# Softmax maxima of the selected and sliding branches from one score pass instead of two

## The chip, the cores and the metric

The kernel runs on one core of a Trainium2 chip. A core has five engines with an instruction queue each, worked off in order: PE (TensorE, matrix products into PSUM), DVE (VectorE), ACT (ScalarE), POOL (GpSimd) and SP (which issues the DMAs). PEld is PE's loading of the stationary operand, shown apart. The metric is the device time of one execution in microseconds (us), as a median of runs; lower is better.

## What is computed

A decoder trunk of two residual layers over 1024 positions with 1024 features, each followed by a SwiGLU block. The change concerns the second layer's sparse attention: 8 heads of 64 features in 2 groups, and for each block of 128 queries three branches, of which two matter here:

```python
q0 = qb * Q_BLOCK
s_s = jnp.einsum('bgrqd,bgqkd->bgrqk', qblk, k_sel) * scale      # selected blocks: 8 of 16, chosen per query
p_s = masked_softmax(s_s, sel_mask)
o_slc = jnp.einsum('bgrqk,bgqkd->bgrqd', p_s, v_sel)
s_w = jnp.einsum('bgrqd,bgkd->bgrqk', qblk, k_band) * scale      # sliding window of 512
p_w = masked_softmax(s_w, w_mask)
o_win = jnp.einsum('bgrqk,bgkd->bgrqd', p_w, v_band)
```

`masked_softmax` subtracts the row maximum before the exponential and divides by the sum.

## The kernel before, in words

All work is recorded as operations first. The class `Order` (L112) then puts them into one order for each engine: a list schedule that takes, on the engine that comes free first, the ready operation with the lowest number. That number is the operation's place in the record plus an offset for its phase from the table `SHIFT` (L47). So the order follows from the record, from `Order`'s own costs, and from the offsets. All instructions are issued from one helper line, L379; the profile tells them apart by tile names.

The stage that matters lies between the projection of the queries (PSUM tile `pcq`) and the output projection (PSUM tile `po`). For every query block qb of 0 to 7 it runs:

- `prep(qb)` (L1173): transposes the block's queries (`pqt`), and makes from them the pair `QQ`. Its first half, QH, is the rounded high part of the query, once in partitions 0 to 63 and once in 64 to 127. Its second half, QL, has the low part in partitions 0 to 63; the rows from 64 carry additive terms: the mask of the selection (rows 64 to 79, blocks 4 to 7 only) and the negated maxima (rows 96 to 111). It also does the compressed branch (`sc`, `ecmp`, `ptc`, `pvc`), the selection (`fcmp`, `pbt`) and its mask.
- `smax(qb, g)` (L1264) for both groups g: the scores of each head with the queries as stationary operand go to PSUM tiles `s` (two buffers), by two products for each bank and branch: QH with `K1` (high part of the keys over their low part) and QL with `K2` (high part of the keys, and constant rows for the additive terms). DVE reduces each bank to a maximum (`mx`), POOL writes the maxima to `nmx`, PE transposes that (`pm`), and ACT writes it into rows 96 to 111 of QL.
- `att(qb, g)` (L1329): the scores again, now transposed (`sT`), with both products and so with the maximum already subtracted; ACT takes the exponential (`pT`), PE multiplies by the values (`pv`), DVE scales and adds into `o`.

Into the same stretch falls DVE's share of the convolution branch, taps of 1024 columns on the tiles `y`, of which 54 stand among the attention's instructions. The pool `t4` (L406) has two buffers; in this stage the last user before the attention is `tq` of the query projection.

Of the kernel before, what the change touches and what calls it, by code (L numbers as in the profile page):

```python
# [9 lines left out]
F32 = mybir.dt.float32  # L10
F32R = mybir.dt.float32r
# [7 lines left out]
P = 128  # L19
# [12 lines left out]
H = 8  # L32
G = 2
R = 4
# [358 lines left out]
def trunk(ctx, tc, x, norm_mix, norm_ffn, ffn_gate, ffn_up, ffn_down, w_in_even, conv_a, pool_w,  # L393
          pool_scale, w_out_even, w_in_odd, q_norm, k_norm, cmp_pos, cmp_w1, cmp_w2, conf_dw,
          conf_dw_b, conf_ln_g, conf_ln_b, w_out_odd, cf32, cb16, k2c, out):
    nc = Order(tc)
# [6 lines left out]
    def unit(shape, name, dt=F32):  # L403
        return data.tile(shape, dt, tag="u8", bufs=NU, name=name)

    def t4(shape, name, dt=F32):  # L406
        return data.tile(shape, dt, tag="t4", bufs=NT4, name=name)
# [4 lines left out]
    def t2(shape, name, dt=F32):  # L412
        return data.tile(shape, dt, tag="t2", bufs=NT2, name=name)
# [359 lines left out]
    for i in range(4):  # L773
# [3 lines left out]
        for h in range(2):  # L777
# [19 lines left out]
            pb = ps1([P, 512], "pb")  # L797
# [134 lines left out]
    K1s, K2s = (unit([P, G, T], n, F32R) for n in ("K1s", "K2s"))  # L932
# [130 lines left out]
    K1w, K2w = (unit([P, G, T], n, F32R) for n in ("K1w", "K2w"))  # L1063
# [104 lines left out]
    def bc(a, n):  # L1168
        return a[:, :, None].to_broadcast([P, a.shape[1], n])

    qstate = {}

    def prep(qb):  # L1173

        gts = gates[:, qb].rearrange("p (h t) -> p h t", t=3)
        QQ = unit([P, 2, H, P], "QQ", F32R)
        o = data.tile([P, H, HD], F32, tag="o", bufs=2, name="o")
        qstate[qb] = QQ, o, gts
        QH, QL = QQ[:, 0], QQ[:, 1]
        nc.gpsimd.memset(QL[64:128].bitcast(F32), 0.0)  # L1180
        p = psn([P, 4, P], "pqt")
        for k in range(4):
            nc.tensor.transpose(p[:, k], Q[qb // 4][:, qb % 4, P * k:P * (k + 1)], ident)
        for u in range(2):
            src = p[64 * u:64 * u + 64]
            own = QH[64 * u:64 * u + 64, u::2]
            nc.scalar.copy(own, src)
            nc.scalar.copy(QH[64 - 64 * u:128 - 64 * u, u::2], src)
            nc.vector.tensor_tensor(QL[0:64, u::2], src, own.bitcast(F32), op=ALU.subtract)
            yield  # L1190

        sc = psn([P, R, G, 64], "sc")
# [2 lines left out]
                         start=True, stop=False)  # L1195
        for r in range(R):
            for g in range(G):
                for s in range(2):
                    nc.tensor.matmul(sc[:, r, g], QQ[:, s, g * R + r], (Kc, Kc2)[s][:, g * 64:(g + 1) * 64],
                                     start=False, stop=r == R - 1 and g == G - 1 and s == 1)  # L1200
# [31 lines left out]
        if qb >= 4:  # L1232
            f = t2([P, 512], "fcmp")
            nc.vector.tensor_tensor(f.rearrange("p (h n) -> p h n", h=H), e, bc(st[:, 8:16], 64), op=ALU.mult)
            nc.vector.scalar_tensor_tensor(f, f, FMIN, f, op0=ALU.is_ge, op1=ALU.mult)
            yield
            w = f[:, 0:256]
            acc = f[:, 0:128]
            nc.vector.tensor_tensor(w, f[:, 0:256], f[:, 256:512], op=ALU.add)
            nc.vector.tensor_tensor(acc, f[:, 0:128], f[:, 128:256], op=ALU.add)  # L1240
            imp = f[:, 128:160].rearrange("p (g j) -> p g j", g=G)
            a4 = acc.rearrange("p (g j k) -> p g j k", g=G, k=4)
            nc.vector.tensor_reduce(imp, a4, axis=AX.X, op=ALU.add)
            nc.vector.tensor_tensor(imp[:, :, 1:], imp[:, :, 1:], a4[:, :, 0:15, 3], op=ALU.add)
            yield
            cA = cf[:, None, C_A + 16 * (qb - 4):C_A + 16 * (qb - 3)].to_broadcast([P, G, 16])
            cB = cf[:, None, C_B + 16 * (qb - 4):C_B + 16 * (qb - 3)].to_broadcast([P, G, 16])
            nc.vector.tensor_tensor(imp, imp, cA, op=ALU.mult)
            nc.vector.tensor_tensor(imp, imp, cB, op=ALU.add)
            yield  # L1250
            top = f[:, 160:176].rearrange("p (g j) -> p g j", g=G)
            left = f[:, 192:224].rearrange("p (g j) -> p g j", g=G)
            for g in range(G):
                nc.vector.max(top[:, g], imp[:, g])
                nc.vector.match_replace(left[:, g], top[:, g], imp[:, g], TAKEN)
            nc.vector.tensor_scalar(selx[:, :, 64:80], left, TAKEN, NEG, op0=ALU.not_equal, op1=ALU.mult)
            yield
            pb = psn([96, G, P], "pbt")
            for g in range(G):
                nc.tensor.transpose(pb[:, g], selx[:, g], ident)  # L1260
            for g in range(G):
                nc.scalar.copy(QL[64:80, R * g:R * (g + 1)], pb[64:80, g, None, :].to_broadcast([16, R, P]))

    def smax(qb, g):  # L1264

        QQ = qstate[qb][0]
        mx = sml(24, "mx", "mx").rearrange("p (b c h) -> p b c h", b=2, c=3)
        if qb >= 4:
            banks = [[(0, qb - 1, 1, 2), (1, qb - 4, 4, 2)]]
            m = qb - 1  # L1270
            banks += [[(0, 0, 1, m)]] if m <= 4 else [[(0, 0, 1, m - 3)], [(0, m - 3, 1, 3)]]
            banks.append([(1, qb - 3, 1, 3)])
        elif qb == 2:
            banks = [[(br, 0, 1, 3)] for br in range(2)]
        else:
            w = min(qb + 1, 2)
            banks = [[(br, k0, 1, w) for br in range(2)] for k0 in range(0, qb + 1, w)]
        for r in range(R):
            h = R * g + r
            used = [0, 0]  # L1280
            for bank in banks:
                ps = ps1([P, 512], "s")
                c0 = 0
                masks = []
                for br, k0, step, n in bank:
                    for s in range(2):
                        end = s == 1 and br == bank[-1][0] and not any(
                            k + (m - 1) * d == qb for _, k, d, m in bank)
                        K = ((K1s, K2s), (K1w, K2w))[br][s]
                        k = K[:, g].rearrange("p (b k) -> p b k", k=P)[:, k0:k0 + (n - 1) * step + 1:step]  # L1290
                        nc.tensor.matmul(ps[:, c0:c0 + n * P].rearrange("p (b k) -> p b k", k=P), QQ[:, s, h], k,
                                         start=c0 == 0 and s == 0, stop=end)
                    if step == 4:
                        masks.append((c0, B_EDGE))
                    if k0 + (n - 1) * step == qb:
                        masks.append((c0 + (n - 1) * P, B_DIAG))
                    c0 += n * P
                if masks:
                    lo = masks[0][0]
                    if len(masks) == 3:  # L1300
                        nc.tensor.matmul(ps[:, lo:c0], identb, cb[:, B_DED:B_DED + 3 * P], start=False, stop=True)
                    else:
                        n = len(masks)
                        o_ = ps[:, :c0].rearrange("p (b k) -> p b k", b=n)[:, :, c0 // n - P:]
                        nc.tensor.matmul(o_, identb, cb[:, None, B_DIAG:B_DIAG + P].to_broadcast([P, n, P]),
                                         start=False, stop=True)
                if len(bank) == 2:
                    nc.vector.tensor_reduce(mx[:, :, used[0], r], ps[:, :c0].rearrange("p (b k) -> p b k", b=2),
                                            axis=AX.X, op=ALU.max)
                    used = [used[0] + 1, used[1] + 1]  # L1310
                else:
                    br = bank[0][0]
                    nc.vector.tensor_reduce(mx[:, br, used[br], r:r + 1], ps[:, :c0], axis=AX.X, op=ALU.max)
                    used[br] += 1
                yield
        if used[0] == 3:
            nc.vector.tensor_tensor(mx[:, 0, 1], mx[:, 0, 1], mx[:, 0, 2], op=ALU.max)
        if used[1] == 2:
            nc.vector.tensor_tensor(mx[:, :, 0], mx[:, :, 0], mx[:, :, 1], op=ALU.max)
        nm = nmx[g]  # L1320
        nv = nm[:, 96:112].rearrange("p (b s h) -> p b s h", b=2, s=2)
        nc.gpsimd.tensor_copy(nv[:, :, 0].bitcast(F32R), mx[:, :, 0])
        nc.gpsimd.tensor_tensor(nv[:, :, 1], mx[:, :, 0], nv[:, :, 0], op=ALU.subtract)
        pm = psn([P, P], "pm")
        nc.tensor.transpose(pm, nm, ident)
        for r in range(R):
            nc.scalar.activation(QQ[96:112, 1, R * g + r], pm[96:112], AF.Copy, scale=cf[96:112, C_DEL + r:C_DEL + r + 1])

    def att(qb, g):  # L1329

        QQ, o, gts = qstate[qb]
        w0 = max(0, qb - 4)
        items = [(0, kb, 0) for kb in range(qb + 1)] + [(1, kb, w0) for kb in range(w0, qb + 1)]
        small = qb == NB - 1 and g == 1
# [25 lines left out]
        for j, (br, kb, k0) in enumerate(items):  # L1360
            if kb == k0:
                pv = psb([P, R, HD + 1], "pv")
            for r in range(R):
                nc.tensor.matmul(pv[:, r], pT[j][:, r], V[:, br, kb, 64 * g:64 * g + 65],
                                 start=kb == k0 and r == 0, stop=kb == qb and r == R - 1)
# [110 lines left out]
```

## Time and profile before

| | us |
|---|---|
| median of 3 runs | 2342.45 (2339.01 to 2343.81) |
| profiled execution | 2341.84 |
| its span | 2339.2 |
| PE busy | 2286.6 (98%) |
| DVE busy | 1450.7 (62%) |
| ACT busy | 720.8 (31%) |
| mean granted clock of PE | 0.992 of 2.4 GHz |

2.6 us of the profiled execution lie outside the span. Shares over the whole run hide the stage in question: from 1230 to 1520 us DVE is nearly as busy as PE, while in the SwiGLU blocks on either side PE is full and DVE is not. A matmul's busy time overlaps that of the next one, so its cost in a full queue is the distance between two starts, not its duration.

### The profile page before, as it was taken

How to read it: one execution, taken by the hardware profiler on the slowest of the kernel's cores; microseconds unless marked ns; L12 is line 12 of the kernel's file. 1: busy time of each engine (PE TensorE's matmuls, PEld its weight loads, DVE VectorE, ACT ScalarE, POOL GpSimd, SP SyncE). 2: the span in 40 equal slices, each digit the busy share in tenths (PEclk: the TensorE clock that was granted, in tenths of full speed). 3: DMA queues.
4: the chain of work that ended last, by engine and by line, in shares of the span. 5: the costliest groups of instructions: out<-in, count | busy, mean ns of one | idle time of the engine just before them, and what ended most of it. 6: DMA issues, size and time to landing. Idle time of an engine off the chain costs nothing.

```text
span 2339.2 us, 27505 instructions
## 1 busy us (share of the span) xinstructions
PE 2286.6 (98%) x11047; PEld 1886.9 (81%) x11047; DVE 1450.7 (62%) x2270; ACT 720.8 (31%) x1253; POOL 77.1 (3%) x116
## 2 busy tenths in 40 slices
PE   7999989999999999999999989999899999999999
PEld 6888868888888888877887878988688888888887
DVE  6444386565656543569999988723865656565432
ACT  4221252222223210324334434632522222232100
POOL 0000000000000000001111000000000000000000
PEclk9999999999999999999999999999999999999999
DMA  5113123222326321322200000032231223262312
GB/s 168 54 63 108 72 82 108 63 82 81 99 63 252 108 100 36 104 64 89 71 22 1 1 1 1 15 112 72 81 108 61 84 81 99 63 242 107 102 37 81
DMA packets 160296, 189.53 MB, mean 81 GB/s; under 512 B 6257, under 2 KB 127017, under 8 KB 160169
## 3 DMA queue, kind: packets, MB, share of 16 engines
q1 hardware_dynamic: 160168, 187.78, 24.4%
q8 instruction: 86, 1.41, 0.3%
q14 instruction: 42, 0.34, 0.0%
HBM read 147.91 MB, written 39.85 MB: 80 GB/s over the span
## 4 chain that ended last, share of the span: by engine, by line
PE 90%; DVE 5%; ACT 2%; issue 1%; DMA 1%; POOL 0%; SPq 0%; ACTq 0%; POOLq 0%; DVEq 0%
PE pd L379 21%; PE pu L379 18%; PE pg L379 18%; PE po L379 7%; PE pv L379 4%; PE s L379 3%; PE sT L379 3%; PE pvv L379 2%; PE pp L379 2%; PE pb L379 2%; PE pcc L379 2%; PE pcq L379 2%; PE pca L379 1%; PE pcb L379 1%; PE pbk L379 1%; DVE y L379 1%
## 5 line engine op out<-in xcount | busy, mean ns | idle before, releaser
L379 PE MATMUL pd<-wd,ah 128*128 128x512 f32 x2112 | 491.2, 394 | 0.0
L379 PEld LDWEIGHTS pd<-wd,ah 128*128 128x128 f32 x2112 | 396.6, 188 | 90.7
L379 DVE TENSOR_TENSOR xf<-pd,xf 128x512 f32<-128x512 f32 x192 | 130.1, 689 | 215.5 <-PE pd L379 215.1
L379 DVE SCALAR_TENSOR_TENSOR y<-z,dwv,y 128x1024 f32<-128x1024 f32 x120 | 153.9, 1283 | 0.8
L379 PEld LDWEIGHTS pv<-V,pT 128*128 128x128 f32 x1056 | 142.7, 193 | 5.9 <-ACT pT L379 0.6
L379 PE MATMUL pg<-T,wgc 128*128 128x512 f32 x528 | 133.0, 398 | 11.6 <-ACT T L379 11.6
L379 PE MATMUL pv<-V,pT 128*128 128x65 f32 x1056 | 138.8, 267 | 0.1
L379 PE MATMUL pg<-B,wga 128*128 128x512 f32 x528 | 130.1, 394 | 2.8 <-ACT pgu L379 2.8
L379 ACT CAST wd<-raw 128x1024 fp32r<-128x1024 f32 x44 | 45.1, 1047 | 282.4 <-PE pd L379 179.7
L379 PE MATMUL pu<-B,wua 128*128 128x512 f32 x528 | 129.8, 394 | 0.0
L379 PE MATMUL pu<-T,wuc 128*128 128x512 f32 x528 | 129.6, 393 | 0.0
L379 PEld LDWEIGHTS pg<-T,wgc 128*128 128x128 f32 x528 | 99.9, 190 | 36.2 <-ACT T L379 12.5
L379 PEld LDWEIGHTS pg<-B,wga 128*128 128x128 f32 x528 | 98.9, 188 | 26.2 <-ACT pgu L379 3.6
L379 PEld LDWEIGHTS pu<-T,wuc 128*128 128x128 f32 x528 | 99.2, 188 | 23.0
L379 PEld LDWEIGHTS pu<-B,wua 128*128 128x128 f32 x528 | 99.0, 188 | 23.2 <-DVE wua L379 0.3
L379 ACT ACTIVATE pT<-sT 128x512 f32<-128x512 f32 x132 | 77.3, 596 | 103.0 <-PE sT L379 102.1
L379 DVE TENSOR_TENSOR act<-pg,pgu 128x512 f32<-128x512 f32 x66 | 45.6, 691 | 91.2 <-PE pg L379 91.0
L379 DVE TENSOR_TENSOR puu<-pu,puu 128x512 f32<-128x512 f32 x88 | 60.9, 692 | 62.9 <-PE pu L379 62.9
L379 DVE TENSOR_REDUCE mx<-s 128x2 f32<-128x512 f32 (+3 forms) x160 | 92.8, 592 | 11.1 <-PE s L379 8.8
L379 PE MATMUL po<-woo,mB 128*128 128x512 f32 x384 | 91.6, 396 | 0.0
L379 PE MATMUL po<-woe,mA 128*128 128x512 f32 x384 | 90.9, 395 | 0.0
L379 PEld LDWEIGHTS po<-woe,mA 128*128 128x128 f32 x384 | 71.6, 188 | 15.9
(331 smaller groups left out, 3957.9 us busy)
## 6 DMA issues: line engine op xcount, KB each, us to landing
raw<-in_ffn_gate_dram SPq DMA_DIRECT2D x44, 512.0 KB, 4.0
rawp<-in_ffn_up_dram SPq DMA_DIRECT2D x44, 512.0 KB, 5.1
actd<-act SPq DMA_DIRECT2D x44, 512.0 KB, 3.0
raw<-in_ffn_down_dram SPq DMA_DIRECT2D x44, 512.0 KB, 4.4
ad<-actd SPq DMA_DIRECT2D x44, 512.0 KB, 6.9
raw<-in_w_in_even_dram SPq DMA_DIRECT2D x16, 512.0 KB, 4.4
xf<-xm SPq DMA_DIRECT2D x8, 1024.0 KB, 10.7
raw<-in_w_in_odd_dram SPq DMA_DIRECT2D x16, 512.0 KB, 3.6
```

The lines of the kernel that those rows point to most:

```text
L379: getattr(getattr(nc, op.eng), op.name)(*op.args, **op.kw)
```

## The change

In `smax`, the maxima are taken from one product for each bank and branch: QH with `K1` for the sliding branch, and for the selected branch of blocks 0 to 3. For the selected branch of blocks 4 to 7 the mask has to be in the scores, so a third form of the queries is made, `QM`: the high part in rows 0 to 63, the selection mask in rows 64 to 79, zero elsewhere, multiplied by `K2`. The scores of `att` keep both products. `QM` takes a buffer of the pool `t4`.

```diff
@@ prep
+        QM = t4([P, H, P], "QM", F32R) if qb >= 4 else None
+        qstate[qb] = QQ, o, gts, QM
...
+        if qb >= 4:
+            nc.gpsimd.memset(QM[64:128].bitcast(F32), 0.0)
...
             nc.vector.tensor_tensor(QL[0:64, u::2], src, own.bitcast(F32), op=ALU.subtract)
+            if qb >= 4:
+                nc.scalar.copy(QM[0:64, u::2], src)
...
                 nc.scalar.copy(QL[64:80, R * g:R * (g + 1)], pb[64:80, g, None, :].to_broadcast([16, R, P]))
+                nc.scalar.copy(QM[64:80, R * g:R * (g + 1)], pb[64:80, g, None, :].to_broadcast([16, R, P]))
@@ smax
-                    for s in range(2):
-                        end = s == 1 and br == bank[-1][0] and not any(
-                            k + (m - 1) * d == qb for _, k, d, m in bank)
-                        K = ((K1s, K2s), (K1w, K2w))[br][s]
...
+                    end = br == bank[-1][0] and not any(k + (m - 1) * d == qb for _, k, d, m in bank)
+                    q, K = (QM[:, h], K2s) if br == 0 and qb >= 4 else (QQ[:, 0, h], (K1s, K1w)[br])
```

`SHIFT` is the same, but the record has fewer operations in `smax` and more in `prep`, so every later operation has another number, and the order changes from the attention on. Up to the first maxima it is the same but for a few instructions.

On PE, the first two banks of `smax` for block 5, group 1. Before (`QQ_1315` is block 5's pair, `cb_71` holds the masks of the diagonal):

```order
L379 MATMUL s_1411<-K1s_879,QQ_1315 128x256
L379 MATMUL s_1411<-K2s_880,QQ_1315 128x256
L379 MATMUL s_1411<-K1w_984,QQ_1315 128x256
L379 MATMUL s_1411<-K2w_985,QQ_1315 128x256
L379 LDWEIGHTS cb_71
L379 MATMUL s_1411<-cb_71 128x384
L379 MATMUL s_1412<-K1s_879,QQ_1315 128x512
L379 MATMUL s_1412<-K2s_880,QQ_1315 128x512
```

and now (`QQ_1316` and `QM_1318` are block 5's):

```order
L379 MATMUL s_1414<-K2s_880,QM_1318 128x256
L379 MATMUL s_1414<-K1w_984,QQ_1316 128x256
L379 LDWEIGHTS cb_71
L379 MATMUL s_1414<-cb_71 128x384
L379 MATMUL pv_1436<-V_881,pT_1431 128x65 x3
L379 MATMUL s_1415<-K2s_880,QM_1318 128x512
```

Two of the four score products of the first bank and one of the two of the second are gone; the product with the masks stays.

On DVE, behind the last maxima of block 5, group 0, up to the low parts of the next block's queries. Before (`y31` are the taps, `mx_1363` the maxima, `QQ_1396` block 6's pair):

```order
L379 TENSOR_TENSOR mx_1363<-mx_1363 128x2x4
L379 RECIPROCAL rs_1386<-pv_1380 128x4
L379 SCALAR_TENSOR_TENSOR y31_1_945<-z31_1042,dwv_85,y31_1_945 128x1024
L379 TENSOR_TENSOR rs_1386<-rs_1386,gates_875 128x4
L379 RECIPROCAL rs_1393<-pv_1388 128x4
L379 SCALAR_TENSOR_TENSOR y31_1_945<-z31_1042,dwv_85,y31_1_945 128x1024
L379 SCALAR_TENSOR_TENSOR o_1252<-pv_1380,rs_1386,o_1252 128x64
L379 SCALAR_TENSOR_TENSOR y31_1_945<-z31_1042,dwv_85,y31_1_945 128x1024
L379 TENSOR_TENSOR QQ_1396<-pqt_1398,QQ_1396 64x4x128
```

and now (`mx_1365` and `QQ_1398` are the same tiles):

```order
L379 TENSOR_TENSOR mx_1365<-mx_1365 128x2x4
L379 RECIPROCAL rs_1388<-pv_1382 128x4
L379 SCALAR_TENSOR_TENSOR y31_1_945<-z31_1042,dwv_85,y31_1_945 128x1024
L379 TENSOR_TENSOR rs_1388<-rs_1388,gates_875 128x4
L379 RECIPROCAL rs_1395<-pv_1390 128x4
L379 SCALAR_TENSOR_TENSOR y31_1_945<-z31_1042,dwv_85,y31_1_945 128x1024
L379 SCALAR_TENSOR_TENSOR o_1252<-pv_1382,rs_1388,o_1252 128x64
L379 SCALAR_TENSOR_TENSOR y31_1_945<-z31_1042,dwv_85,y31_1_945 128x1024
L379 SCALAR_TENSOR_TENSOR o_1252<-pv_1382,rs_1388,o_1252 128x64
L379 SCALAR_TENSOR_TENSOR y31_1_945<-z31_1042,dwv_85,y31_1_945 128x1024
L379 TENSOR_TENSOR QQ_1398<-pqt_1401,QQ_1398 64x4x128
```

One more tap stands between the maxima and the first subtraction; nothing else of DVE's work is added or removed in the stage.

On ACT, the copies that make block 5's queries out of the transposed tile. Before (`pT` are exponentials of `att`):

```order
L379 CAST QQ_1315<-pqt_1317 64x4x128 x3
L379 ACTIVATE pT_1341<-sT_1340 128x512
L379 CAST QQ_1315<-pqt_1317 64x4x128
L379 ACTIVATE pT_1341<-sT_1342 128x512
L379 ACTIVATE pT_1341<-sT_1344 128x512
```

and now:

```order
L379 CAST QQ_1316<-pqt_1319 64x4x128 x2
L379 CAST QM_1318<-pqt_1319 64x4x128
L379 CAST QQ_1316<-pqt_1319 64x4x128 x2
L379 CAST QM_1318<-pqt_1319 64x4x128
L379 ACTIVATE pT_1343<-sT_1342 128x512
```

The copy to `QM` stands ahead of the second pair of copies to `QQ`, on which DVE's second subtraction waits.

## Rows read from the trace of the kernel before

**Rows 1.** The page, chain that ended last, by engine.

```profile
PE 90%; DVE 5%; ACT 2%; issue 1%; DMA 1%; POOL 0%; SPq 0%; ACTq 0%; POOLq 0%; DVEq 0%
```

**Rows 2.** Busy time by stretch: start:end, length, busy time and count per engine.

```profile
core 0: us, PE busy (x) PEld busy (x) DVE busy (x) ACT busy (x) POOL busy (x), PEclk, DMA share, GB/s
1230.45:1436.10 205.65, 193.44 (x1337) 167.94 (x1336) 188.23 (x417) 86.83 (x185) 20.94 (x30) 0.96 0.00 1
1436.10:1491.22 55.12, 55.12 (x408) 51.67 (x406) 46.77 (x115) 32.20 (x60) 2.11 (x8) 1.00 0.00 1
1491.22:1520.02 28.80, 28.80 (x204) 26.22 (x202) 19.70 (x48) 17.77 (x34) 0.72 (x3) 1.00 0.10 25
1520.02:1652.60 132.58, 132.58 (x723) 112.34 (x723) 50.47 (x90) 47.84 (x76) 4.64 (x9) 1.00 0.25 91
```

**Rows 3.** Tile s on PE, whole span: count, ns min/median/max, first and last start, forms.

```profile
L379 PE MATMUL s<-K2s,QQ x120: 272/284/423, 1229.6 to 1512.6; 128*128 128x256 f32 x64, 128*128 128x384 f32 x40, 128*128 128x128 f32 x8, 128*128 128x512 f32 x8
L379 PE MATMUL s<-K2w,QQ x104: 273/281/422, 1229.8 to 1518.5; 128*128 128x256 f32 x56, 128*128 128x384 f32 x40, 128*128 128x128 f32 x8
```

**Rows 4.** Tile s on PE, from 1436.10 to 1520.02.

```profile
L379 PE MATMUL s<-K2s,QQ x48: 276/308/342, 1436.1 to 1512.6; 128*128 128x256 f32 x24, 128*128 128x384 f32 x24
L379 PE MATMUL s<-K2w,QQ x32: 278/308/422, 1436.4 to 1518.5; 128*128 128x256 f32 x16, 128*128 128x384 f32 x16
```

**Rows 5.** Tile s on PE, from 1436.10 to 1491.22.

```profile
L379 PE MATMUL s<-K2s,QQ x37: 276/283/342, 1436.1 to 1490.9; 128*128 128x256 f32 x21, 128*128 128x384 f32 x16
L379 PE MATMUL s<-K2w,QQ x25: 278/282/343, 1436.4 to 1491.2; 128*128 128x256 f32 x13, 128*128 128x384 f32 x12
```

**Rows 6.** Timeline of PE: start us, us, engine, line, operation.

```profile
1442.11 0.33 PE L379 MATMUL s<-K1w,QQ 128*128 128x384 f32 x1
1442.28 0.34 PE L379 MATMUL s<-K2w,QQ 128*128 128x384 f32 x1
...
1442.80 0.28 PE L379 MATMUL s<-K2s,QQ 128*128 128x256 f32 x1
1442.92 0.29 PE L379 MATMUL s<-K1w,QQ 128*128 128x256 f32 x1
1443.04 0.28 PE L379 MATMUL s<-K2w,QQ 128*128 128x256 f32 x1
```

**Rows 7.** DVE's waits, 1230.45 to 1436.10: us in total, times, longest.

```profile
DVE QQ L379 <- ACT QQ L379: 9.0, 8, 3.9
DVE mx L379 <- PE s L379: 3.1, 11, 0.4
DVE rs L379 <- PE pv L379: 2.2, 3, 1.2
DVE stcm L379 <- ACT ecmp L379: 1.5, 1, 1.5
```

**Rows 8.** Groups by form, 1230.45 to 1436.10: count, busy us, mean ns, idle before.

```profile
L379 ACT CAST QQ<-pqt 64x512 fp32r<-64x512 f32 x24 | 13.9, 580 | 8.7 <-PE pqt L379 6.5 <-DVE QQ L379 1.5
...
L379 POOL MEMSET QQ<- 64x1024 f32 x6 | 5.6, 949 | 0.2
...
L379 ACT CAST QQ<-pbt 16x512 fp32r<-16x512 f32 x6 | 3.2, 574 | 3.0 <-PE pbt L379 3.0
```

**Rows 9.** Timeline behind the maxima of block 5, group 0; in brackets the idle time.

```profile
1397.59 1.25 DVE L379 SCALAR_TENSOR_TENSOR y<-z,dwv,y 128x1024 f32<-128x1024 f32 x1
1397.71 1.18 POOL L379 CAST nmx<-mx 128x8 fp32r<-128x8 f32 x1 [22.43 <-DVE rs L379]
...
1400.30 0.33 PE L379 MATMUL pm<-cf,nmx 128*128 128x128 f32 x1 [3.36 <-POOL nmx L379]
...
1404.18 0.68 DVE L379 TENSOR_TENSOR QQ<-pqt,QQ 64x512 fp32r<-64x512 f32 x1 [2.62 <-ACT QQ L379]
```

**Rows 10.** Busy time by stretch, from the maxima of block 5, group 0, to those of group 1.

```profile
1397.71:1436.10 38.39, 32.86 (x186) 26.95 (x187) 33.13 (x74) 15.55 (x29) 3.90 (x3) 0.82 0.00 1
```

**Rows 11.** DVE's waits, 1436.10 to 1491.22.

```profile
DVE mx L379 <- PE s L379: 4.8, 8, 1.1
```

More of the change, by code (lines that the diff above doesn't have):

```diff
@@ L1177, in prep @@
         o = data.tile([P, H, HD], F32, tag="o", bufs=2, name="o")
-        qstate[qb] = QQ, o, gts
+        QM = t4([P, H, P], "QM", F32R) if qb >= 4 else None
+        qstate[qb] = QQ, o, gts, QM
         QH, QL = QQ[:, 0], QQ[:, 1]
         nc.gpsimd.memset(QL[64:128].bitcast(F32), 0.0)
+        if qb >= 4:
+            nc.gpsimd.memset(QM[64:128].bitcast(F32), 0.0)
         p = psn([P, 4, P], "pqt")
@@ L1262, in prep @@
                 nc.scalar.copy(QL[64:80, R * g:R * (g + 1)], pb[64:80, g, None, :].to_broadcast([16, R, P]))
+                nc.scalar.copy(QM[64:80, R * g:R * (g + 1)], pb[64:80, g, None, :].to_broadcast([16, R, P]))
     def smax(qb, g):
-        QQ = qstate[qb][0]
+        QQ, QM = qstate[qb][0], qstate[qb][3]
         mx = sml(24, "mx", "mx").rearrange("p (b c h) -> p b c h", b=2, c=3)
@@ L1285, in smax @@
                 for br, k0, step, n in bank:
-                    for s in range(2):
-                        end = s == 1 and br == bank[-1][0] and not any(
-                            k + (m - 1) * d == qb for _, k, d, m in bank)
-                        K = ((K1s, K2s), (K1w, K2w))[br][s]
-                        k = K[:, g].rearrange("p (b k) -> p b k", k=P)[:, k0:k0 + (n - 1) * step + 1:step]
-                        nc.tensor.matmul(ps[:, c0:c0 + n * P].rearrange("p (b k) -> p b k", k=P), QQ[:, s, h], k,
-                                         start=c0 == 0 and s == 0, stop=end)
+                    end = br == bank[-1][0] and not any(k + (m - 1) * d == qb for _, k, d, m in bank)
+                    q, K = (QM[:, h], K2s) if br == 0 and qb >= 4 else (QQ[:, 0, h], (K1s, K1w)[br])
+                    k = K[:, g].rearrange("p (b k) -> p b k", k=P)[:, k0:k0 + (n - 1) * step + 1:step]
+                    nc.tensor.matmul(ps[:, c0:c0 + n * P].rearrange("p (b k) -> p b k", k=P), q, k,
+                                     start=c0 == 0, stop=end)
                     if step == 4:
@@ L1329, in att @@
     def att(qb, g):
-        QQ, o, gts = qstate[qb]
+        QQ, o, gts = qstate[qb][:3]
         w0 = max(0, qb - 4)
```

## The prediction

> **What bounds the kernel now.** I read the page first. Its chain of waits is nearly all PE [rows 1], so at first sight any PE time that goes is a gain. Then I read the busy times by stretch around the attention, cut where the maxima of a group are done [rows 2]. Call A the stretch up to the maxima of block 5, group 1 (205.65 us), B1 the next, up to those of block 7, group 0 (55.12), B2 the one up to the last maxima (28.80), and C the rest up to the SwiGLU block (132.58). In A, PE is busy 193.44 and idle 12.2, but DVE is busy 188.23: the two engines have almost the same load. In B1 and B2 PE has no idle time at all, DVE 46.77 of 55.12 and 19.70 of 28.80. In C, PE is full and DVE has little. So PE sets the pace from B1 on; in A the pace is set by both, with DVE only 5.2 us of work behind PE. Third, I read what DVE waits for in A [rows 7]: 9.0 us for ACT's copies of the queries, 3.1 and 2.2 for PE, 1.5 for ACT's exponential.
>
> **What the change removes.** 120 + 104 second products [rows 3], each with its weight load. In a full queue one costs the distance of two starts: 0.17 us for 384 columns (1442.11 to 1442.28), 0.12 for 256 (1442.80 to 1442.92 to 1443.04) [rows 6]. The 128-column form I price like 256 (0.12, an upper bound), the 512-column form by columns (0.23, an estimate from the 384 row). That is 120 x 0.12 + 80 x 0.17 + 16 x 0.12 + 8 x 0.23 = 14.4 + 13.6 + 1.9 + 1.8 = 31.7 us of PE. The part behind A is 40 x 0.12 + 40 x 0.17 = 11.6 [rows 4], of it 34 x 0.12 + 28 x 0.17 = 8.8 in B1 [rows 5], so 2.8 in B2 and 20.1 in A.
>
> **Stretch A.** PE would have 193.4 - 20.1 = 173.3 us of work, DVE still 188.2: the reductions stay, one for each bank, and and the order shows all 54 taps, as before, ahead of block 5's last maximum. So DVE becomes the bound, and what A can give is only what DVE waits for PE. Bounds: all 17.4 us of DVE's idle time stay, gain 0 (below nothing by the added work that follows); or PE's share (5.3) and half of ACT's 9.0 go, since ACT in its turn waits for PE's transposes, gain about 10. I take PE's share alone, 5.3, because the longest waits for ACT follow a loop that the change does not cut: behind the last maximum, POOL's cast takes 1.18 us next to a tap, PE waits 3.36 for the transpose of the maxima, the next block's queries are queued behind it on PE, and DVE waits 2.62 for ACT's copy of these [rows 9]. In the new order the same instructions stand in this place, with one more tap of DVE's to cover the wait: 1.2 us off at block 5.
>
> **What is added.** Per block from 4 to 7, two copies of the query and two of the mask on ACT, 0.58 and 0.57 each, and one memset on POOL of 0.95 [rows 8]; in all 16 x 0.58 = 9.2 us of ACT, which is busy 86.8 of 205.65 in A [rows 2], so its time as such is hidden. What is not: the first `QM` copy stands ahead of the copy on which DVE's second subtraction waits, so that wait grows by up to 0.58 for blocks 4, 5 and 6 in A (1.7 us) and for 7 in B1 (0.6); at the least nothing, if ACT finishes them under DVE's tap. I take it whole. The memsets for blocks 6 and 7 stand on POOL ahead of the casts of block 4's and block 5's maxima of group 1, and need the buffer of `QM` two blocks earlier, which is free only when the last selected scores of that very group are done. Each can delay the maxima by 0 to 0.95; I take half, 0.9 together. The memsets of blocks 4 and 5 come early, where PE is behind. ACT's exponentials stand up to 1.2 us later where two `QM` copies are ahead of them; `att` has two score tiles under way and PE has spare time in A, so I price that at nothing; without the cover it is 1.2 x 4 = 4.8 us.
>
> A: 5.3 + 1.2 - 1.7 - 0.9 = 3.9 us gained.
>
> **Stretches B and C.** In B1, PE falls to 55.1 - 8.8 = 46.3, DVE stays at 46.8: a tie. DVE's idle time there is 8.3, of which 4.8 is waiting for PE's scores [rows 11]. Bounds: gain 0 if waits of DVE on other engines take their place, 8.3 if DVE runs through. I take the 4.8, less 0.6 for block 7's copy: 4.2. In B2, PE goes from 28.8 to 26.0 and DVE has 19.7, so the 2.8 shows. C has no `s` products: nothing, and the SwiGLU blocks have the same instructions.
>
> Sum: 3.9 + 4.2 + 2.8 = 10.9 us of 31.7. The profiled execution took 2341.84 us (span 2339.2 and 2.6 around it), 0.6 less than the median of the runs shown. So 2341.8 - 10.9 = 2330.9, I say **2331 us**. Its own range: A from 0 to 10, B1 from 0 to 8.3, B2 2.8, so 2320 to 2339.
>
> **Rivals.**
>
> *DVE binds throughout.* DVE keeps its idle time in A and B1, and the PE time removed turns into PE waiting. For: the tie in B1, the near tie in A, and that PE, arriving earlier at each transpose of the maxima, waits longer there with the next block's queries queued behind. Against: 5.3 and 4.8 us of DVE's waits are for PE and nothing else [rows 7, 11]. Then only B2's 2.8 is gained, and the added 1.7 + 0.6 + 0.9 is paid: 2342 us.
>
> *PE's time shows in full.* For: the chain is 90% PE [rows 1]. Against: DVE's 188.2 us in A are more than PE's 173.3 would be; no order can shorten them. 2341.8 - 31.7 = 2310 us.
>
> *The clock falls.* This one is slower. PE's waits for the maxima grow, and the clock goes down behind them. Behind the 3.36 us wait of block 5 [rows 9] the granted clock was 0.82 over 38.39 us [rows 10], a mix of 2.4 and 1.2 GHz: 0.18 x 38.4 = 6.9 us of full clock lost. In A after the change PE has 201.7 - 173.3 = 28.4 us without work, of which it needs 12.2 for the waits that it has now, so 16.2 to lose. Two more such stretches are hidden; from the third, PE sets the pace of A again, and from the fourth (27.6 us, more than 16.2 + 10.9) the kernel is slower. With six: 41.4 - 16.2 - 10.9 = 14.3 us slower, 2356 us. For: PE will have more than twice the idle time in A, at eleven transposes of maxima. Against: the mean clock over A was 0.96 with 12.2 us of idle time [rows 2], so the other waits cost little clock, and the new idle time comes partly in small pieces, for the two `s` buffers.
>
> The Trainium skill, TensorE: Matmul & The Clock Gate, section "What's actually happening", speaks against the change in the same sense: the clock is gated by default, and only activity of the array releases it, so fewer products can cost clock. By that rule the time is this last rival's. The trace agrees in one place, [rows 10]; everywhere else in the stage PE's waits cost it little clock.
>
> **How the numbers follow.** My forecast 0.73, DVE throughout 0.13, PE in full 0.04, the clock 0.10. A measurement of this kernel can tell about 0.2%, 4.7 us, from no change; so faster is below 2337.8. Of the forecast's range 2320 to 2339 only the end lies above that (0.03 of its 0.73). Faster: 0.73 - 0.03 + 0.04 = 0.74; same: 0.13 + 0.03 = 0.16; slower 0.10. The range reaches up over the second case and down a little below the forecast's own, 2318 to 2343, and leaves out PE in full and the clock, 0.14, and some of the tails.
>
> **What would show it.** In the profile after: 224 products of the tile `s` fewer on PE; in the stretch up to the maxima of block 5, group 1, about 188 us of DVE busy in about 202, and PE's idle time there up from 12 to 25 or 30 us, ended by POOL's `nmx`; DVE's waits for `s` and `pv` nearly gone, those for ACT's `QQ` still there at 9 or 10 us; B1 some 51 us and B2 some 26. The forecast is wrong if DVE's busy time in A is not near 188, if its waits for ACT go too (then the gain is nearer 20), or if the granted clock over A falls below some 0.9.

## The result and the profile after

The changed kernel took 2366.7 us, median of 4 runs (2360.7 to 2370.9), against 2342.1 before: a ratio of 1.0105 (95% interval 1.0077 to 1.0133). It is 24.6 us slower; the forecast was 10.9 us faster. The profiled execution is the fastest of the four, 2360.7 us with a span of 2358.9, so the trace shows 19.7 us of the loss.

The page's chain of waits looks as it did [rows 1], and so would mislead again:

```profile
PE 89%; DVE 6%; ACT 3%; issue 1%; DMA 1%; POOL 0%; SPq 0%; ACTq 0%; DVEq 0%; POOLq 0%
```

Tile `s` on PE in the kernel after (count, ns min/median/max, first and last start, forms), beside [rows 3]:

```profile
L379 PE MATMUL s<-K1w,QQ x104: 273/283/881, 1229.4 to 1533.6; 128*128 128x256 f32 x56, 128*128 128x384 f32 x40, 128*128 128x128 f32 x8
L379 PE MATMUL s<-K2s,QM x80: 280/397/774, 1327.6 to 1528.0; 128*128 128x256 f32 x40, 128*128 128x384 f32 x32, 128*128 128x512 f32 x8
L379 PE MATMUL s<-K1s,QQ x40: 222/366/562, 1229.3 to 1319.1; 128*128 128x256 f32 x24, 128*128 128x128 f32 x8, 128*128 128x384 f32 x8
```

The change does what it says: 224 products are gone. The median of the selected ones, 397 ns, is not to be read against the 284 of [rows 3]: those were the second products of a bank. The first ones, whose place the new products take, took a mean of 349 ns at 256 columns before (`K1s`, all blocks) and take 385 now (`K2s` with `QM`, blocks 4 to 7): part of them ran at the lower clock. The same four stretches as in [rows 2], cut at the same casts on POOL:

```profile
1230.40:1447.82 217.42, 189.79 (x1207) 162.12 (x1205) 188.54 (x419) 92.75 (x197) 25.08 (x34) 0.88 0.00 1
1447.82:1514.84 67.02, 58.36 (x344) 51.31 (x343) 49.50 (x120) 34.07 (x64) 2.18 (x8) 0.82 0.00 1
1514.84:1534.88 20.04, 19.77 (x136) 17.38 (x135) 15.00 (x32) 15.89 (x29) 0.39 (x2) 1.00 0.07 27
1534.88:1672.70 137.82, 137.82 (x760) 116.86 (x760) 53.38 (x96) 49.66 (x79) 4.64 (x9) 1.00 0.25 88
```

A is 11.8 us longer, B1 11.9, B2 8.8 shorter, C 5.2 longer (B2's count of products falls and C's rises: work has moved behind the last maxima). Over all four, PE is idle 36.6 us where it was 12.2, and busy 405.7 where it was 410.0, though the products taken out were priced at 31.7. So 24.4 us more waiting, and 27.5 us of the saving gone while PE is busy: the clock column says why (0.88 and 0.82, before 0.96 and 1.00). PE's waits up to the last maxima (total, times, longest), before and then after:

```profile
PE pm L379 <- POOL nmx L379: 6.0, 3, 3.4
PE sT L379 <- ACT pT L379: 2.2, 3, 1.0
PE pqt L379 <- ACT QQ L379: 1.5, 2, 1.2
```

```profile
PE pm L379 <- POOL nmx L379: 10.3, 4, 6.6
PE s L379 <- ACT QM L379: 5.9, 1, 5.9
PE sT L379 <- ACT pT L379: 4.9, 6, 2.8
PE sc L379 <- ACT QM L379: 4.3, 1, 4.3
PE sc L379 <- DVE QQ L379: 3.1, 2, 1.7
PE pqt L379 <- ACT QQ L379: 2.7, 3, 1.2
```

Two of the waits name `QM`, which the prediction had priced by ACT's time alone. And the stretches of the kernel after in which the clock was low, cut at single casts (before, only block 4's with 0.94 and [rows 10] with 0.82):

```profile
1293.98:1323.58 29.60, 27.86 (x177) 25.22 (x176) 22.75 (x64) 13.25 (x25) 1.34 (x3) 0.83 0.00 1
...
1342.61:1376.74 34.13, 28.65 (x171) 25.75 (x171) 26.69 (x64) 13.71 (x27) 3.30 (x3) 0.80 0.00 1
...
1401.89:1447.82 45.93, 36.83 (x184) 29.79 (x184) 36.68 (x81) 17.41 (x33) 4.47 (x4) 0.72 0.00 1
...
1461.85:1489.01 27.16, 25.67 (x157) 23.68 (x157) 17.81 (x52) 11.47 (x22) 0.39 (x2) 0.81 0.00 1
1489.01:1514.84 25.83, 19.02 (x100) 16.08 (x100) 18.51 (x42) 14.53 (x26) 1.40 (x4) 0.74 0.01 1
```

Length times what is missing to 1.00, these lose 5.0 + 6.8 + 12.9 + 5.2 + 6.7 = 36.6 us of full clock; before it was 1.8 + 6.9 = 8.7. (An upper measure: it counts the lower clock while PE is idle, too.) The 27.9 more are what the rival "the clock falls" needed for the kernel to be slower at all (16.2 + 10.9 = 27.1), not for 24.6 us. The question is what made it fall: the missing products, the copies for `QM`, or the new order of everything.

### The profile page after: what moved, and what is told of

Same layout as the page of the kernel before. It is cut to its first block, busy times and chain, and to the rows that moved or that the text cites. A ratio compares the mean times of both kernels' runs of the same rounds, so it can differ in the third digit from the quotient of the medians.

```text
span 2358.9 us, 27087 instructions
## 1 busy us (share of the span) xinstructions
PE 2283.4 (97%) x10823; PEld 1876.5 (80%) x10823; DVE 1451.9 (62%) x2270; ACT 728.6 (31%) x1269; POOL 81.1 (3%) x120
## 4 chain that ended last, share of the span: by engine, by line
PE 89%; DVE 6%; ACT 3%; issue 1%; DMA 1%; POOL 0%; SPq 0%; ACTq 0%; DVEq 0%; POOLq 0%
PE pd L379 21%; PE pu L379 18%; PE pg L379 18%; PE po L379 7%; PE pv L379 4%; PE sT L379 3%; PE pvv L379 2%; PE pp L379 2%; PE pb L379 2%; PE pcc L379 2%; PE s L379 2%; PE pcq L379 2%; PE pca L379 1%; PE pcb L379 1%; PE pbk L379 1%; DVE y L379 1%
## 5 line engine op out<-in xcount | busy, mean ns | idle before, releaser
L379 PEld LDWEIGHTS pv<-V,pT 128*128 128x128 f32 x1056 | 155.2, 207 | 6.3
L379 PE MATMUL pv<-V,pT 128*128 128x65 f32 x1056 | 149.2, 280 | 0.0
## 6 DMA issues: line engine op xcount, KB each, us to landing
xf<-xm SPq DMA_DIRECT2D x8, 1024.0 KB, 10.8
```

The lines of the kernel that those rows point to most:

```text
L379: getattr(getattr(nc, op.eng), op.name)(*op.args, **op.kw)
```

## The experiments

Three theories: ORDER (the planner, given less work, put the instructions in another order, and its table of priorities had been set for the old one), COPIES or BANK (what making `QM` holds up), CLOCK (PE with less work loses its clock). Ratios are against the kernel before, run beside each.

**Changed work in the old order.** The planner sees the dropped products (`ghost`) as before, and `QM`'s memset and copies (`extra`) as taking no time; the instructions then stand in exactly the order of before.

```diff
+        if self.extra:
+            op.occ = op.dur = 0.0
...
+                        nc.ghost = s != sel
+                if op.ghost:
+                    continue
```

> The changed kernel's work, issued in exactly the order of the kernel before: the dropped products keep their place in the planner's record and are only left out when the instructions are issued, and the copies and memsets for QM stand directly behind their neighbours at no cost to the planner. Theory ORDER (the priorities were set for the old record; in the new order PE meets waits that it did not have): with the old order the change shows its gain, 2325 to 2338 us, and the long waits of the kernel after (6.65 us for the maxima of block 5, 5.90 for the mask of block 7, 4.26 at block 5's compressed scores) go. Theory COPIES (the QM copies hold the bank of the transposed queries and put the mask later, wherever they stand): 2352 to 2365 us, with PE's waits for ACT's QM still there. Theory CLOCK (any PE time taken out of this stage is paid back as lower clock): 2355 us or more, granted clock of the whole run at 0.98 or below.

2343.2 us, 1.0002 (0.9992 to 1.0013). The order alone is worth 23.5 us of the 24.6; the change is then no loss, but no gain either. None of the three theories had this time in its range: ORDER had expected a gain, so something else takes it.

**The products put back in the new order.**

```diff
+                for a in op.first:
+                    nc.tensor.matmul(*a, start=True, stop=True)
```

> The changed kernel in its own order, but with a second product of the same shape issued ahead of each one for the maxima, into the same bank, overwritten by the real one: the 224 products are back as pure PE work, 31.7 us at full clock. ORDER: the order is the fault and the work comes on top, 2366 us at the least, up to 2395. COPIES: likewise no faster than the changed kernel, 2360 to 2390. CLOCK: PE is busier in the stage, its clock stays up as before and the time falls back to 2340 to 2352.

2374.1 us, 1.0142 (1.0128 to 1.0156). 7.4 us slower than the changed kernel: CLOCK as the whole cause is out. But 31.7 us of work cost only 7.4. Its low-clock stretches lose 5.3 + 13.3 + 5.1 = 23.7 us (0.85 over 35.28, 0.72 over 47.35, 0.81 over 26.61), against 36.6 without the products. By these two profiles 12.9 us of the lost clock go with the missing products and 15.0 with the order and the copies. The sizes are rough, since each is from one execution; the direction holds in all: 1 less the mean clock, times the span, is 31 to 38 us in the 4 runs with the products, 45 to 59 in the 4 without, and 14 to 23 in the kernel before.

**`QM` made in the kernel before, and not read.** Old order, both products; `smax` as before.

```diff
-                    q, K = (QM[:, h], K2s) if br == 0 and qb >= 4 else (QQ[:, 0, h], (K1s, K1w)[br])
+                        nc.tensor.matmul(ps[:, c0:c0 + n * P].rearrange("p (b k) -> p b k", k=P), QQ[:, s, h], k,
```

> The kernel before, in its own order and with both products, and QM made beside it but not read by any product: 4 memsets on POOL, 16 copies on ACT. COPIES: 2352 to 2365 us, and PE waits where the compressed scores need the bank of the transposed queries. ORDER: 2342 to 2346, the copies are nearly hidden. CLOCK: 2342 to 2346, since PE has all its work.

2351.1 us, 1.0040 (1.0026 to 1.0053): the copies cost 9.0 us, a little less than COPIES said, where the prediction had 3.2. From here to the first run the products are taken out: 7.9 us.

The trace shows what the copies do. Preparation of block 6 in the kernel before, from DVE's first subtraction on [rows 9 has that row]: ACT's next exponential, and the score product of PE that waits for it.

```profile
1404.18 0.60 ACT L379 ACTIVATE pT<-sT 128x512 f32<-128x512 f32 x1
1404.83 0.79 PE L379 MATMUL sT<-QQ,K1s 128*128 128x512 f32 x1 [1.03 <-ACT pT L379]
```

The same with `QM` made beside it:

```profile
1409.94 0.68 DVE L386 TENSOR_TENSOR QQ<-pqt,QQ 64x512 fp32r<-64x512 f32 x1 [2.77 <-ACT QQ L386]
1410.66 0.58 ACT L386 CAST QM<-pqt 64x512 fp32r<-64x512 f32 x1 [0.75 <-DVE QQ L386]
1411.14 0.59 ACT L386 ACTIVATE pT<-sT 128x512 f32<-128x512 f32 x1
1411.79 0.80 PE L386 MATMUL sT<-QQ,K1s 128*128 128x512 f32 x1 [2.23 <-ACT pT L386]
1412.84 0.58 ACT L386 CAST QM<-pqt 64x512 fp32r<-64x512 f32 x1
1413.45 0.69 DVE L386 TENSOR_TENSOR QQ<-pqt,QQ 64x512 fp32r<-64x512 f32 x1 [1.63 <-ACT QM L386]
```

ACT's first copy to `QM` waits 0.75 for DVE's subtraction, and DVE's second subtraction 1.63 for ACT's second copy, though both only read `pqt` and share no other tile: they take turns at it. The exponential that stands behind the copy on ACT comes 1.2 us later (0.75 of waiting and 0.48 of the copy), and so does PE's product: it waits 2.23 instead of 1.03. The Trainium skill, PSUM — Partial Sum Buffer, section "PSUM bank collisions raise a hardware error", states it: a compiler adds a dependency between instructions of two engines on the same part of a bank, two reads included. The trace agrees. The prediction had overlooked it; a sign of it stood in [rows 8], where 1.5 us of the idle time of ACT's copies end with DVE.

Over the stage, ACT's copies to `QM` wait 3.8 us for DVE, and DVE's subtractions 3.1 for these copies:

```profile
L386 ACT CAST QM<-pqt 64x512 fp32r<-64x512 f32 x8 | 4.6, 580 | 3.8 <-DVE QQ L386 3.8
L386 DVE TENSOR_TENSOR QQ<-pqt,QQ 64x512 fp32r<-64x512 f32 x14 | 9.6, 688 | 15.9 <-ACT QQ L386 12.8 <-ACT QM L386 3.1
```

PE waits 6.2 us for exponentials where it waited 2.2:

```profile
PE sT L386 <- ACT pT L386: 4.9, 4, 2.2
PE pv L386 <- ACT pT L386: 1.3, 2, 0.8
```

And the whole stage, A to C, before and with `QM`:

```profile
1230.40:1652.60 422.20, 409.99 (x2665) 358.22 (x2664) 305.22 (x667) 184.65 (x353) 28.46 (x48) 0.98 0.09 31
1230.40:1662.11 431.71, 414.00 (x2666) 361.38 (x2665) 305.73 (x667) 192.70 (x369) 31.23 (x52) 0.97 0.09 30
```

It is 9.5 us longer: PE is idle 5.5 us more, and busy 4.0 more with the same products, at a lower clock.

**One product only where no `QM` is needed.** Old order; sliding scores and blocks 0 to 3, 144 products dropped.

```diff
+                    both = br == 0 and qb >= 4
+                        nc.ghost = s == 1 and not both
```

> The order of the kernel before; one product for all sliding scores and for the selected scores of blocks 0 to 3 (144 products dropped), two products for the selected scores of blocks 4 to 7, and no QM at all. ORDER and COPIES both: 2328 to 2340 us. CLOCK: 2350 or more, lower clock in the stage though nothing is added.

2334.3 us, 0.9966 (0.9955 to 0.9978), as ORDER and COPIES said.

**`QM` from SBUF.** Old order, all 224 products dropped; the query rows of `QM` come by one copy out of `QQ`.

```diff
-            if qb >= 4:
-                nc.scalar.copy(QM[0:64, u::2], src)
+            if u and qb >= 4:
...
+                nc.scalar.copy(QM[0:64], QH[0:64].bitcast(F32))
```

> As the run with the work of the changed kernel in the order of before, except that QM's query rows are not copied from the transposed queries in PSUM (two copies of 64x512 for each block) but by one copy of 64x1024 from the high part that lies in SBUF. Theory BANK (ACT's copies and DVE's subtractions take turns at the bank of the transposed queries, so each QM copy between them puts off the subtraction and the release of the bank; this is what the 9 us of QM alone consist of): 2334 to 2339 us, and ACT's QM copies wait for DVE no more. Theory ACT TIME (the copies cost because ACT is late with exponentials and masks; the copy is no shorter now): 2341 to 2348.

2331.9 us, 0.9961 (0.9948 to 0.9973): 11.3 us from this line, against the first run, and 2 below BANK's range. BANK holds, not ACT TIME: the one copy is no shorter (1.05 us), but off the tile. At block 6 the exponential follows the first copies at once, and PE waits 1.03 again:

```profile
1398.04 0.60 ACT L386 ACTIVATE pT<-sT 128x512 f32<-128x512 f32 x1
1398.69 0.79 PE L386 MATMUL sT<-QQ,K1s 128*128 128x512 f32 x1 [1.03 <-ACT pT L386]
...
1400.59 1.05 ACT L386 CAST QM<-QQ 64x1024 fp32r<-64x1024 f32 x1
```

Over the stage PE's score products wait 2.5 us for exponentials, where they waited 5.2 in the first run. The edit also moves the copy, behind the last one of `QQ`; the turns seen in the trace speak for the tile, but no run changes the place alone.

**The old numbers, true times.** The dropped products still take up a number in the record.

```diff
-            op.grp = op.seq + self.shift.get(op.phase, 0)
+            op.grp = op.num + self.shift.get(op.phase, 0)
```

> The changed kernel with the record numbers of before: each dropped product still takes up a number, QM's operations take none, so that the priorities of all other operations are those of before; the planner's times are the true ones. Theory NUMBERS (the 204 numbers that are gone shift every operation against the table of priorities): 2340 to 2350 us, near the run in the order of before (2343). Theory TIMES (the planner, knowing that PE has less to do, sees other operations ready first and puts them otherwise): 2356 to 2372, near the changed kernel (2367).

2365.1 us, 1.0100 (1.0086 to 1.0114). The numbers alone don't bring the old time back: with the planner's true times the order is slow even so.

**Another table.** `SHIFT` replaced by one under which the planner ends earlier (two of its entries here).

```diff
-'smax70': -1663, 'prep7': -479
+'smax70': -2644, 'prep7': -3334
```

> The changed kernel with another table of priorities, found by a search in which the planner's own end of the program was made as early as it would go. ORDER: if the loss lies in the table, another one repairs it at least in part, 2335 to 2352 us. If the planner doesn't see what makes the new order slow (turns at a bank, the cast on POOL beside a tap, the clock), a table that it likes is no better: 2356 to 2375.

2361.6 us, 1.0101 (1.0083 to 1.0118). Three orders that the planner made for the changed work all lie between 2361 and 2367: the planner's model doesn't see what costs here.

**`QM` from SBUF in the new order.** The edit as above, in the issue order of the changed kernel, where the copy stands behind the last one of `QQ`.

```diff
+                    last.late = QM[0:64], QH[0:64].bitcast(F32)
...
+                if op.late:
+                    nc.scalar.copy(*op.late)
```

> The changed kernel in its own order, but QM's query rows come from the high part in SBUF by one copy behind the last copy of the transposed queries, in place of two copies out of PSUM. BANK: the 11 us that this gave in the order of before come here too, 2353 to 2358 us. If the waits of the new order cover them: 2361 to 2367.

2353.6 us, 1.0048 (1.0036 to 1.0060): 13.1 us less than the changed kernel, BANK again. What is left to the same work in the old order, 21.7, is the order's.

**Single places of the new order.** First, ACT's copies of block 7's mask moved forward; then one score product of block 5.

```diff
+                    op.hoist = qb == 7
...
+            op.hoist = (qb, g, j) == (5, 0, 4)
...
+                ops.remove(op)
+                ops.insert(max(ops.index(d) for d in op.deps) + 1, op)
```

> The changed kernel, with one thing moved: ACT's four copies of block 7's selection mask (two for QQ, two for QM) stand right behind the transposes that they read, ahead of the 11 activations of group 1's maxima and of the normalisation that stood before them. PLACES (the 23 us of the new order are a few waits, this the largest but one: PE waits 5.90 us for QM's mask, and its clock is 0.74 up to the next maxima): the wait goes, 2354 to 2362 us, and the stretch from block 6's last maxima to block 7's first falls from 25.8 to 16 or 19. If the copies only hand the delay on to ACT's normalisation and so to PE's sums: 2363 to 2369.

> The changed kernel, with one thing moved: in block 5's group 0 one second score product of the attention (tile sT) stands right behind its first, ahead of the 12 value products that stood between them and took 5.2 us; ACT's exponentials waited 9.3 us there, and DVE 3.8 for the exponential of the compressed scores behind them. PLACES: DVE's wait goes and the stretch between block 5's maxima falls from 45.9 by 3 to 7, 2360 to 2364 us. If DVE's wait only moves: 2365 to 2369.

2368.4 (1.0112; 1.0099 to 1.0125) and 2365.2 us (1.0099; 1.0081 to 1.0117): nothing. In the first, PE's wait for the mask became one of 7.23 us for DVE, whose maxima also stood behind the normalisation:

```profile
1507.64 0.69 PE L384 MATMUL s<-K2s,QM 128*128 128x384 f32 x1 [7.23 <-DVE mx L384]
```

So the next moves the whole of block 7's preparation (`QM` from SBUF, 2353.6 to compare with):

```diff
-'prep7': -479
+'prep7': -879
```

> The changed kernel with QM's query rows from SBUF (2354 us), and the preparation of block 7 given a priority 400 numbers earlier, with which the planner puts the mask of block 7 ahead of the last maxima of block 6 and the normalisation between the maxima of block 7, as in the order of before; all that stands earlier is unchanged. PLACES: the stretch between block 6's last maxima and block 7's first falls from 25.8 to some 16 us, 2343 to 2349 in all. If the normalisation then delays what follows by as much: 2351 to 2356.

2342.1 us, 1.0002 (0.9993 to 1.0012), 11.5 us of the 21.7. The stretch from block 6's last maxima to block 7's first, before the move and after it:

```profile
1483.05:1508.83 25.78, 19.04 (x100) 16.09 (x100) 18.49 (x42) 14.52 (x26) 1.39 (x3) 0.74 0.00 1
```

```profile
1482.61:1497.44 14.83, 14.83 (x101) 13.02 (x101) 14.10 (x28) 13.73 (x26) 0.39 (x3) 1.00 0.01 2
```

PE's instructions are nearly the same (100 and 101), with 6.7 us less waiting and the clock at 2.4 GHz throughout. Of DVE's, 14 with 4.4 us of busy time now stand elsewhere.

**The clock behind block 5's wait.** Products that nobody reads fill PE's waits for the maxima, in the old order without `QM`, in the old order with `QM` from SBUF, in the new order, and in the new order with block 7 earlier.

```diff
+        op.fill = [(pf, QQ[:, 0, R * g], K1s[:, g, 0:512])] * FILL.get((qb, g), 0)
```

> As the run without QM in the order of before (2334), but PE does products that nobody reads, of 512 columns each, in front of the transposes of the maxima of group 0 of block 5 (14) and block 4 (6), into the bank of that transpose, where it waited 3.43 and 1.62 us. CLOCK (what such a wait costs is mostly the lower clock behind it): the granted clock from block 5's wait to the next maxima rises from 0.78 to 0.95 or more and the time falls to 2323 to 2331 us. If the wait itself is the cost and the clock behind it is hidden by other engines: 2333 to 2339, whatever the clock does. If the filling runs longer than the wait, it is slower by as much, up to 4 us.

> The fastest two edits together: the order of before, one product for all maxima, QM's query rows from SBUF (2332), and the waits of PE for the maxima of group 0 of blocks 5 and 4 filled with 16 and 7 products of 512 columns that nobody reads. CLOCK: 1.6 us come back in block 4 and 1 to 3 in block 5, 2326 to 2330 us. If the filling gains nothing beside what differs from run to run: 2331 to 2334.

> The changed kernel in its own order, QM's query rows from SBUF (2354 us), with PE's waits for the maxima of group 0 of block 5 (6.65 us), of block 4 (1.22) and of group 1 of block 3 (1.45) filled with 26, 5 and 6 products of 512 columns that nobody reads. CLOCK: behind block 5's wait the granted clock was 0.60 over 52 us, against 0.78 over 38 in the order of before; with the wait filled it stays higher, the stretch falls to 40 to 45 us and the run to 2341 to 2347. If the low clock of that stretch comes from the waits behind it, or costs nothing: 2350 to 2356.

> The two edits together: block 5's wait filled and block 7 prepared earlier, QM's query rows from SBUF. If the clock behind block 5 and the normalisation ahead of block 7 are what the new order costs, 2331 to 2339 us, within a few us of the order of before (2332). If either of them only moves the loss: 2341 to 2349.

2331.8 (0.9956; 0.9944 to 0.9969), 2329.2 (0.9948; 0.9936 to 0.9960), 2356.1 (1.0049; 1.0033 to 1.0064) and 2345.6 us (1.0012; 1.0003 to 1.0022). In the old order 2.5 and 2.7 us less than unfilled, with intervals that overlap, though the runs of the second pair don't (2327.7 to 2329.9 against 2331.0 to 2335.0); in the new order 2.5 and 3.5 more, again with intervals that overlap. The clock of block 5's stretch only rose from 0.78 to 0.86, not to 0.95. In the new order the runs spread from 2344.5 (clock 0.987) to 2364.0 (0.979); the profile is of the shortest, and its block 5 is like that of the changed kernel's profile, which had no filling (45.93, 0.72), so it shows nothing of the filling:

```profile
1390.60:1436.24 45.64, 38.32 (x193) 30.97 (x191) 36.68 (x81) 17.11 (x32) 4.47 (x4) 0.78 0.00 1
```

**The taps.** The new order has 9 taps behind block 5's first maxima, the old one 6. Block 7 earlier, and the last set of taps moved to block 3.

```diff
-'conv32': -38
+'conv32': -438
```

> As the run with block 7 prepared earlier (2342 us), but the last set of taps given a priority 400 numbers earlier: the planner then puts 15 taps in place of 6 between the maxima of block 3's two groups, and none in place of 9 between those of block 5. TAPS (the taps left over behind block 5's first maxima delay the normalisation and keep DVE, and so PE, waiting): the stretch of block 5 falls from 46 to some 38 us; what block 3 then takes longer is at most 9 x 1.28 = 11.5 us, less what DVE had free there (7 of 30): 2334 to 2340. If the taps cost the same wherever they stand: 2341 to 2348.

> The same with 200 numbers: 13 taps between the maxima of block 3, 10 for block 4's second group, 12 and 3 at block 5 (the order of before has 9, 8, 12 and 6). TAPS: 2334 to 2340. If the taps cost the same wherever they stand, or the planner's changes further on outweigh them: 2341 to 2350.

2343.0 (1.0001; 0.9992 to 1.0010) and 2345.8 us (1.0012; 1.0003 to 1.0020; with -238): no gain over 2342.1. With all 9 taps moved block 5's stretch fell from 46 to 33, but block 3's grew from 27 to 39 and the one up to block 5's first maxima from 25 to 36; the taps only carry the loss along.

## Why the prediction was wrong

The two steps that failed:

- "In the new order the same instructions stand in this place." The prediction looked at the places on which its terms rest and took the rest of the new order at no price. Even in this place, where it counted 1.2 us off, PE's wait for the maxima grew from 3.4 to 6.6 us. Three pairs of runs give the order's price: 2366.7 against 2343.2, 2374.1 against 2351.1, 2353.6 against 2331.9, that is 21.7 to 23.5 us, whatever the products and however `QM` is made; and two other planned orders are no better. 11.5 us of it lie at block 7, whose mask the planner put behind the normalisation on ACT and DVE. The other 10 lie by the stretches in blocks 4 and 5; neither the filled wait nor the taps nor the single product accounts for them. What makes them is open.
- "... so that wait grows by up to 0.58", with the memsets 1.7 + 0.6 + 0.9 = 3.2 us, and for the exponentials behind the copies "I price that at nothing". Measured: 9.0 added alone, 11.3 and 13.1 given back by taking the copies off the tile in PSUM (and behind the last copy of `QQ`). The term counted the copies' time on ACT, and not the turns that ACT and DVE take at the tile. These put the exponentials off, and PE waits 4.0 us more for them, near the 4.8 that the prediction named "without the cover" and dropped; the lower clock takes about as much again.

What held: with these two out (old order, `QM` from SBUF) the forecast's stretches come close. A, B1, B2 and C of that run:

```profile
1230.40:1429.58 199.18, 182.02 (x1188) 150.29 (x1187) 185.47 (x414) 92.07 (x193) 23.59 (x34) 0.95 0.00 1
1429.58:1481.65 52.07, 50.93 (x349) 44.19 (x348) 46.10 (x115) 34.95 (x65) 2.11 (x8) 1.00 0.00 1
1481.65:1509.25 27.60, 27.06 (x182) 23.32 (x182) 19.33 (x48) 17.43 (x33) 0.71 (x2) 1.00 0.10 24
1509.25:1641.71 132.46, 132.46 (x722) 112.20 (x722) 50.54 (x90) 47.72 (x76) 4.64 (x9) 1.00 0.26 91
```

A gains 6.5 (forecast 3.9), B1 3.1 (4.2), B2 1.2 (2.8), C 0.1: 10.8 before rounding, beside the 10.9 summed. That the sums agree is luck: the errors of 2.6, 1.1 and 1.6 cancel, and without the three terms that this run doesn't have (1.2 for the new order's tap, 1.7 and 0.6 for the copies out of PSUM) the forecast would have been 12.0. The mechanism in A is borne out: DVE is busy 185.5 of 199.2 us, its waits for `s` are gone, those for ACT's `QQ` are 7.9 us where they were 9.0, and most of the 31.7 us stays hidden, as said. In the changed kernel itself DVE's 188.5 us and PE's 27.6 us idle in A are what the forecast named, but three of its signs are not there: A is 217 us long, not 202; DVE's waits for `s` and `pv`, which were to be nearly gone, are 6.6 and 2.5 us where they were 3.1 and 2.2; and the granted clock over A is 0.88, below the 0.9 that it gave as a sign of being wrong.

The rivals: "DVE binds throughout" and "PE's time shows in full" both assumed the order's waits unchanged, and fell with it. "The clock falls" was the right side; that its 2356 us is near the 2367 measured is luck. It counted six more stretches of low clock, 41.4 us. The trace has 27.9 more, which by its own sum is 0.8 us slower; the rest is PE's longer waiting, 24.4 us. Its cause was only in part the one given. With the products missing, the old order kept and `QM` from SBUF, the stretches lose 0.06 x 29.9 + 0.22 x 38.2 = 10.2 us of full clock, 1.5 more than before. In the old order with the copies out of PSUM they lose 22.4 us without the products (the first run) and 13.5 with them (the third). So the missing products cost clock where PE has more to wait for, be it by the new order (12.9) or by the copies (8.9); all of these are from single profiles. The Trainium skill, TensorE: Matmul & The Clock Gate, section "What's actually happening", says that activity releases the clock; these pairs of runs agree. The tenth that the prediction gave the rival was too little because the waits that a new order makes were left out.

A version that beats both kernels came out of it: old order, one product, `QM` from SBUF and the two waits filled, 2329.2 us; without the filling 2331.9.

## What to carry to other kernels

Where a scheduler orders the work by a table that was set for the old record, a change of the record is two changes: try its work in the old order first (keep what is dropped as a place holder), and only then let the scheduler loose. A copy added on a second engine is priced by the tile that it reads in PSUM: who else reads that tile, and what stands behind the copy on its own engine. And read the granted clock by stretch when a dense engine has waits: here 24.4 us more of waiting went with 27.5 us of the saving lost while PE was busy at the lower clock.

## What was not expected of the hardware

The same instructions ran at quite different clocks from one execution to the next. The new order's stretch between block 5's maxima took 45.9 us at 0.72 in the changed kernel's profile, and in the profile with block 7's mask moved, which has the same instructions there, this:

```profile
1402.52:1454.66 52.14, 43.37 (x182) 36.46 (x183) 37.38 (x80) 17.41 (x33) 4.46 (x4) 0.60 0.00 0
```

The changed kernel's four runs follow the clock: 2360.7 us at a mean of 0.981, 2363.5 at 0.979, 2369.9 at 0.976 and 2370.9 at 0.975. So one profile of such a kernel doesn't tell a stretch's clock; several do.
